# ConvFFN's gate and up projections as two-by-two block products with seven multiplications, in a pass of their own

## The chip, the cores and the metric

One core of one Trainium2 chip runs the kernel. The metric is the time of one execution on the device in microseconds (us); the kernel before took 3261.3 us, the median of 3 runs (3259.72 to 3262.79). Engines are called as in the profile: PE multiplies matrices, PEld loads its weights, DVE, ACT and POOL work on vectors, SP issues DMA transfers.

## The reference

Two layers of a diffusion trunk work on 1024 latent tokens (a 16 x 64 grid) and 128 context tokens with 1024 channels. Layer 0 has a mixer of gated DeltaNet and retention heads, layer 1 a Hyena mixer; each mixer ends in an output projection that is added to the residual x. Behind each stands a ConvFFN with 2816 inner channels, which the change is about:

```python
def conv_ffn(h, w_gate, w_up, w_conv, b_conv, w_down, on_grid):
    gate = h @ w_gate
    up = h @ w_up
    gate = dwconv2d_grid(gate, w_conv) if on_grid else dwconv1d(gate, w_conv[1])
    return (jax.nn.silu(gate + b_conv) * up) @ w_down
...
        hc = modulate(rmsnorm(xc, norm2[l]), mc[3], mc[4])
        hl = modulate(rmsnorm(xl, norm2[l]), ml[3], ml[4])
        xc = xc + mc[5] * conv_ffn(hc, *ffn, on_grid=False)
        xl = xl + ml[5] * conv_ffn(hl, *ffn, on_grid=True)
```

The gate passes a 3x3 depthwise convolution on the grid (three taps on the context). All data is float32.

## The kernel before, in words

Channels lie on the 128 partitions, the 1152 tokens along the free dimension, in NG = 3 groups of G = 384. Every large product is made of three matmuls (`mm3`, lines 134 to 136): each operand is split into a rounded part (hi) and the rest (lo), and hi x hi, hi x lo and lo x hi are summed in PSUM. A weight block is loaded by SP, cast to hi on ACT (line 125) and its lo is a subtraction on DVE (line 126, `wsplit`).

`ffn` (from line 378) goes over 22 blocks of 128 inner channels. `gate(m)` and `up(m)` each run `project`: 3 token groups x 8 blocks of input channels x 3 matmuls of 384 columns. ACT copies the gate out of PSUM (line 384); `conv` does the convolution with 8 instructions of DVE over the grid (line 402) and 2 over the context (line 407), and Silu on ACT. The result of `up` is multiplied in from PSUM on DVE (line 417) and split into hi and lo (lines 418, 419), which stay in SBUF. After each group of blocks (GROUPS, line 37: six groups of up to four) the down projection of that group runs, 8 output blocks x 3 token groups, and `add_x` (line 374) adds each result, scaled, to the residual x in SBUF. The last group goes token group by token group, and the normalisation that follows (`norm_after` or `final`) goes in between.

Ahead of `ffn` stand `out_begin` and `out_end` (lines 802, 849): the mixer's output projection (8 output blocks x 3 token groups x 24 matmuls), `rstd` (line 273; squares on ACT, sums on DVE, a reciprocal root by Newton steps) and `norm_h` (line 305), which writes the normalised, modulated and split operand h. Its scaling on DVE is line 316, splits are lines 321 to 327, some on POOL. The operand of the output projection itself is split at lines 821 and 822. Line 777 is part of the Hyena stage.

`fill` is a list of small pieces of work for the next layer, taken off one at a time by `filler` after each projection and in the down loops: 48 blocks of the modulation (`mod_parts`, line 225; DVE lines 243 and 246) and 8 pieces of the Hyena filter (lines 563 to 569). The order of instructions on each engine is fixed when the kernel is built, from the order in which they are written down and from when their buffers and operands are expected to be ready; buffers come from pools with a fixed number of tiles per tag. All DMA is issued by SP in one order.

## Time and profile before

| | |
|---|---|
| median of 3 runs | 3261.3 us |
| profiled execution, its own time | 3267.89 us |
| its span, first to last instruction | 3266.1 us |
| mean granted TensorE clock | 0.988 of full speed |
| PE, DVE, ACT, POOL busy | 97%, 74%, 32%, 11% |
| first ConvFFN, about | 974 to 1820 us |
| second ConvFFN, about | 2425 to 3252 us |

Times in the trace count from the span's start. A line number is that of the kernel before; where a helper such as `mm3` records every matmul, all stand under its lines, and the names of the tiles (`psg<-hh,wh` is written to PSUM tile `psg` from operand `hh` and weights `wh`) tell them apart. Matmuls overlap in the trace, so the distance between starts is their pace and not the duration of one.

### The profile page before, as it was taken

Reading aid. Unit: us, or ns where it says so; the run is one execution under the profiler, and the core shown is the slowest. Engines: PE = TensorE matmul, PEld = TensorE weight load, DVE = VectorE, ACT = ScalarE, POOL = GpSimd, SP = SyncE. Lnnn points to the kernel's source line nnn. Section 1 sums busy time; section 2 is a strip of 40 time slices with the busy share of each in tenths; the row PEclk is TensorE's granted clock in tenths of the full one; section 3 lists DMA queues with packets and bytes.
Section 4 is the critical chain, followed back from the end, with each engine's and each line's share of the span. In section 5 each row is a group of like instructions: output and inputs, shape, how many; then the busy total and the mean of one; then the engine's idle time right before and its main releaser. Section 6 shows DMA issues by size and latency. Waiting matters only on the chain.

```text
span 3266.1 us, 50005 instructions
## 1 busy us (share of the span) xinstructions
PE 3163.2 (97%) x19856; PEld 3027.5 (93%) x19856; DVE 2406.2 (74%) x5016; ACT 1051.5 (32%) x1889; POOL 369.8 (11%) x406
## 2 busy tenths in 40 slices
...
GB/s 209 69 30 62 62 43 83 39 80 74 131 14 64 90 93 84 78 84 90 79 44 53 179 101 100 109 79 101 154 19 47 39 46 39 46 41 44 45 40 71
DMA packets 84830, 241.38 MB, mean 74 GB/s; under 512 B 10274, under 2 KB 33264, under 8 KB 84596
## 3 DMA queue, kind: packets, MB, share of 16 engines
...
q14 instruction: 78, 0.64, 0.1%
...
## 4 chain that ended last, share of the span: by engine, by line
PE 65%; DVE 7%; issue 1%; DMA 1%; ACT 1%; POOL 0%; DVEq 0%; SPq 0%; ACTq 0%; POOLq 0%
PE psg L134 15%; PE psg L136 15%; PE psg L135 15%; PE psu L134 6%; PE psu L135 6%; PE psu L136 6%; PE psu L656 0%; PE psu L659 0%; PE psu L657 0%; PE psu L658 0%; DVE t L496 0%; PE psu L297 0%; DVE t L497 0%; PE pss L290 0%; DVE x L777 0%
## 5 line engine op out<-in xcount | busy, mean ns | idle before, releaser
L135 PE MATMUL psg<-hl,wh 128*128 128x384 f32 x2400 | 820.0, 342 | 2.7 <-POOL hl L327 2.5
L134 PE MATMUL psg<-hh,wh 128*128 128x384 f32 x2400 | 817.4, 341 | 4.3 <-ACT hh L321 2.6
L136 PE MATMUL psg<-hh,wl 128*128 128x384 f32 x2400 | 818.1, 341 | 0.0
L134 PEld LDWEIGHTS psg<-hh,wh 128*128 128x128 f32 x2400 | 452.7, 189 | 7.3 <-ACT hh L321 3.2
L135 PEld LDWEIGHTS psg<-hl,wh 128*128 128x128 f32 x2400 | 452.9, 189 | 5.6 <-POOL hl L327 5.0
L136 PEld LDWEIGHTS psg<-hh,wl 128*128 128x128 f32 x2400 | 453.1, 189 | 0.0
L402 DVE SCALAR_TENSOR_TENSOR t<-t,vec,t 128x945 f32<-128x945 f32 (+2 forms) x352 | 427.2, 1217 | 23.4 <-ACT t L390 23.4
L125 ACT CAST wh<-wr 128x1024 fp32r<-128x1024 f32 (+1 forms) x192 | 198.6, 1034 | 722.1 <-PE psg L135 627.1
L126 DVE TENSOR_TENSOR wl<-wr,wh 128x1024 fp32r<-128x1024 f32 (+1 forms) x190 | 229.6, 1208 | 255.8 <-ACT wh L125 255.5
L374 DVE SCALAR_TENSOR_TENSOR x<-psg,mod,x 128x384 f32<-128x384 f32 (+2 forms) x444 | 218.0, 513 | 236.4 <-PE psg L136 235.2
L134 PE MATMUL psu<-hh,wh 128*128 128x384 f32 x1056 | 353.0, 334 | 0.0
L136 PE MATMUL psu<-hh,wl 128*128 128x384 f32 x1056 | 353.0, 334 | 0.0
L135 PE MATMUL psu<-hl,wh 128*128 128x384 f32 x1056 | 352.9, 334 | 0.0
L136 PE MATMUL psg<-t,wl 128*128 128x384 f32 x960 | 321.7, 336 | 2.1 <-DVE wl L126 2.1
L134 PE MATMUL psg<-t,wh 128*128 128x384 f32 x960 | 321.7, 335 | 0.0
L135 PE MATMUL psg<-t,wh 128*128 128x384 f32 x960 | 321.4, 335 | 0.0
L134 PEld LDWEIGHTS psu<-hh,wh 128*128 128x128 f32 x1056 | 198.2, 188 | 1.2 <-ACT t L384 0.6
L136 PEld LDWEIGHTS psu<-hh,wl 128*128 128x128 f32 x1056 | 198.2, 188 | 0.8 <-issue 0.6
L135 PEld LDWEIGHTS psu<-hl,wh 128*128 128x128 f32 x1056 | 198.2, 188 | 0.6 <-issue 0.6
L136 PEld LDWEIGHTS psg<-t,wl 128*128 128x128 f32 x960 | 180.9, 188 | 2.5 <-DVE wl L126 2.5
L134 PEld LDWEIGHTS psg<-t,wh 128*128 128x128 f32 x960 | 180.6, 188 | 0.8 <-issue 0.6
L135 PEld LDWEIGHTS psg<-t,wh 128*128 128x128 f32 x960 | 180.6, 188 | 0.0
...
## 6 DMA issues: line engine op xcount, KB each, us to landing
...
```

What stands on the lines that cost most here:

```text
L125: nc.scalar.copy(hi, raw)
L126: (eng or nc.vector).tensor_sub(lo, raw, hi.bitcast(F32))
L134: nc.tensor.matmul(out, lhsT=wh, rhs=xh, start=first and i == 0, stop=False)
L135: nc.tensor.matmul(out, lhsT=wh, rhs=xl, start=False, stop=False)
L136: nc.tensor.matmul(out, lhsT=wl, rhs=xh, start=False, stop=last and i == n - 1)
L374: nc.vector.scalar_tensor_tensor(out=self.x[ob][:, c0:c1], in0=p[:, o], scalar=g, in1=self.x[ob][:, c0:c1], op0=ALU.mult, op1=ALU.add)
L402: nc.vector.scalar_tensor_tensor(out=o, in0=gs[:, r0 + di : r1 + di, c0 + dj : c1 + dj], scalar=w(i, j), in1=o, op0=ALU.mult, op1=ALU.add)
```

## The change

The gate block and the up block of the same 128 inner channels are computed together. The weights are a two-by-two matrix of blocks (rows of the two halves of the input channels; columns gate and up), and h is one too (the two halves of the input channels; even and odd tokens). Instead of the eight products of such a pair, seven are made of sums of blocks (PRODUCTS), and the four results are sums of the seven.

- `out_begin` and `out_end` work on quarters of Q = 288 tokens instead of thirds; weights are loaded and split again for each use. x is kept in halves (`xhalf`) and saved to DRAM (`mid_x`). `norm_ops` takes the place of `norm_h`: it makes B11, B21, B22 and T1 to T4 out of h (four differences per pair of channel blocks, on DVE and POOL) and splits each.
- `pair_weights` loads a gate and an up block and makes S1 to S4 on POOL (three differences and a sum); it splits three tiles of 1024 columns (two on POOL, one on DVE) and one of 512.
- `pair_products` runs the seven products, each over 4 channel blocks x 3 matmuls of 288 columns for one or both halves of the tokens, and sums them: the first is copied out of PSUM on ACT, the others are added from PSUM on DVE, into `y1` (gate) and `y2` (up), every second token.
- `ffn` becomes two passes. The first goes over all 22 blocks (the first two of them in halves), runs `conv`, multiplies by `up` on POOL and stores the product to DRAM (`mid`). The second reads `mid` back, splits it, and runs the down projection in four groups (GROUPS); x is read back too. The fillers are taken three at a time in the down loops of the first three groups, and nowhere else.
- PSUM has 3 + 4 + 1 banks in ConvFFN (3 + 3 + 2 before); weights come from one pool of 9 tiles; `dynamic_dma_scratch_size` goes from 8192 to 1024. `w_down` is laid out in blocks of 128.

```diff
+Q = T // 4
+QP = Q // 2
-NT2 = 7
-NE = 6
+NT2 = 6
+NE = 7
+NW = 9
+NS = 4
-GROUPS = [(0, 2), (2, 6), (6, 10), (10, 14), (14, 18), (18, 22)]
+GROUPS = [(0, 8), (8, 12), (12, 18), (18, 22)]
+
+B11, B21, B22, T1, T2, T3, T4 = range(7)
+PRODUCTS = {1: ("g", "A11", B11), 2: ("u", "A12", B21), 6: ("g", "S2", T2), 3: ("u", "S4", B22),
+            7: ("g", "S3", T3), 4: ("u", "A22", T4), 5: ("u", "S1", T1)}
...
     def open_t2(self, es):
         self.pt2 = es.enter_context(self.tc.tile_pool(name="pt2", bufs=NT2))
+        self.pw = es.enter_context(self.tc.tile_pool(name=self.n("pw"), bufs=NW))
+        self.one = True
+
+    def W(self, shape, dt=F32):
+        return self.pw.tile(list(shape), dt, tag="w", name=self.n("w"))
...
+    def rstd(self, n, order=range(NB), tag="u", pool=(), w=G):
         accs = {}
...
+    def new_ops(self, s):
+
+        def new(t, u):
+            if t == "h":
+                return [self.ph.tile([128, 4, Q], F32R, tag=x, name=self.n("o")) for x in ("hh", "hl")]
+            return [self.pt.tile([128, 4, Q], F32R, tag="t", name=self.n("o")), self.pt2.tile([128, 4, Q], F32R, tag="t2", name=self.n("o"))]
+
+        a = new("h", 0)
+        self.ops[s] = {}
+        for k in range(4):
+            self.ops[s][B11, k] = [t[:, k : k + 1] for t in a]
+        for pair, tags in (((B21, B22), "hh"), ((T1, T3), "ht"), ((T2, T4), "tt")):
+            for h in range(2):
+                t = [x.rearrange("p (k o) c -> p k o c", k=2) for x in new(tags[h], h)]
+                for k in range(2):
+                    self.ops[s][pair, 2 * h + k] = [x[:, k] for x in t]
+                    for o in range(2):
+                        self.ops[s][pair[o], 2 * h + k] = [x[:, k, o : o + 1] for x in t]
+
+    def norm_ops(self, l, which, q, r):
+
+        nc = self.nc
+        s, off = q // 2, QP * (q % 2)
+        if q % 2 == 0:
+            self.new_ops(s)
+        a = self.modA[:, 2 * l + which]
+        sh = self.mod[:, l, 3 * which]
+        v, g = nc.vector, nc.gpsimd
+        for k in range(4):
+            x = []
+            for b in (k, 4 + k):
+                tmp = self.E([128, G])[:, :Q]
+                for c0, c1, st in streams(q * Q, q * Q + Q):
+                    o = slice(c0 - q * Q, c1 - q * Q)
+                    v.scalar_tensor_tensor(out=tmp[:, o], in0=self.xcols(b, c0, c1), scalar=a[:, b, st : st + 1],
+                                           in1=r[:, o], op0=ALU.mult, op1=ALU.mult)
+                    nc.scalar.activation(out=tmp[:, o], in_=tmp[:, o], func=AF.Identity, bias=sh[:, b, st : st + 1])
+                x.append(tmp.rearrange("p (c e) -> p e c", e=2))
+            ta, tb = [self.E([128, G])[:, :Q].rearrange("p (e c) -> p e c", e=2) for _ in range(2)]
+            v.tensor_sub(ta[:, 0], x[0][:, 1], x[0][:, 0])
+            g.tensor_sub(ta[:, 1], x[1][:, 1], x[0][:, 1])
+            v.tensor_sub(tb[:, 0], x[1][:, 1], ta[:, 0])
+            g.tensor_sub(tb[:, 1], x[1][:, 0], tb[:, 0])
+            for key, raw, eng in ((B11, x[0][:, 0:1], v), ((B21, B22), x[1], g), ((T1, T3), ta, v), ((T2, T4), tb, v)):
+                hi, lo = [t[:, :, off : off + QP] for t in self.ops[s][key, k]]
+                self.split(raw, hi, lo, eng)
+
...
+    def pair_weights(self, g_src, u_src):
+
+        nc = self.nc
+        u, g, d = [self.W([128, NB, 128]) for _ in range(3)]
+        nc.sync.dma_start(u, u_src)
+        nc.sync.dma_start(g, g_src)
+        h = [slice(0, 4), slice(4, 8)]
+        sm = lambda dt=F32: self.pw.tile([128, 4, 128], dt, tag="s", bufs=NS, name=self.n("s1"))
+        s1 = sm()
+        e = nc.gpsimd
+        e.tensor_add(s1, u[:, h[0]], u[:, h[1]])
+        e.tensor_sub(d[:, h[0]], s1, g[:, h[0]])
+        e.tensor_sub(d[:, h[1]], g[:, h[1]], d[:, h[0]])
+        e.tensor_sub(u[:, h[0]], g[:, h[0]], u[:, h[0]])
+        s1 = self.split(s1, sm(F32R), sm(F32R), nc.vector)
+        g, d, u = [self.split(t, self.W([128, NB, 128], F32R), self.W([128, NB, 128], F32R), eng)
+                   for t, eng in ((g, e), (d, nc.vector), (u, e))]
+        part = lambda t, i: (t[0][:, h[i]], t[1][:, h[i]])
+        return {"S1": s1, "A11": part(g, 0), "A12": part(g, 1), "S2": part(d, 0), "S4": part(d, 1),
+                "S3": part(u, 0), "A22": part(u, 1)}
+
+    def pair_products(self, w, cols, y1, y2):
+
+        nc = self.nc
+        sums = {s: self.E([128, G])[:, :Q] for s in cols}
+        half = lambda y, s, e: y[:, 2 * Q * s + e : 2 * Q * (s + 1) : 2]
+        add = nc.vector.tensor_add
+        for i, (tag, name, op) in PRODUCTS.items():
+            wh, wl = w[name]
+            for s in cols:
+                p = self.psum(tag, [128, Q])
+                x = self.op(op, s)
+                self.mm3(p, [((wh[:, k], wl[:, k]), x[k]) for k in range(4)])
+                t = sums[s]
+                if i == 1:
+                    nc.scalar.copy(t, p)
+                elif i == 2:
+                    add(half(y1, s, 0), p, t)
+                elif i in (6, 7):
+                    add(t, p, t)
+                elif i == 3:
+                    add(half(y1, s, 1), p, t)
+                elif i == 4:
+                    add(half(y2, s, 0), p, t)
+                else:
+                    add(half(y2, s, 1), p, t)
+                    add(half(y1, s, 1), p, half(y1, s, 1))
...
-        def up(m, acc):
-            hi, lo = self.T(F32R), self.T2(F32R)
-
-            def evac(n, p):
-                c = slice(n * G, n * G + G)
-                nc.vector.tensor_mul(acc[:, c], acc[:, c], p)
-                nc.scalar.copy(hi[:, c], acc[:, c])
-                nc.vector.tensor_sub(lo[:, c], acc[:, c], hi[:, c].bitcast(F32))
-
-            self.project(self.A["w_up"][l, m], "u", evac)
-            return hi, lo
-        gs = [gate(m) for m in range(2)]
-        self.project_first(gs[0][1], gs[1][1])
-        accs = {m: conv(m, gs[m][0]) for m in range(2)}
+
+        mid = self.pd.tile([NFB, 128, T], F32, name=self.n("mid"))
+        plan = [(0, (0,)), (1, (0,)), (0, (1,)), (1, (1,))] + [(m, (0, 1)) for m in range(2, NFB)]
+        blocks, units = {}, []
+
+        def prepare():
+            if len(units) < len(plan):
+                m, cols = plan[len(units)]
+                if m not in blocks:
+                    blocks[m] = (self.X(), self.X())
+                w = self.pair_weights(self.A["w_gate"][l, m], self.A["w_up"][l, m])
+                units.append((w, cols, *blocks[m]))
+
+        prepare()
+        yield
+        for k, (m, cols) in enumerate(plan):
+            prepare()
+            self.pair_products(*units[k])
+            units[k] = None
+            if cols[-1] == 1:
+                g, u = blocks.pop(m)
+                acc = conv(m, g)
+                nc.gpsimd.tensor_mul(acc, acc, u)
+                nc.sync.dma_start(mid[m], acc)
+
+
+        def mids(gi):
+            m0, m1 = GROUPS[gi]
+            out = []
+            for m in range(m0, m1):
+                if gi % 2 == 0:
+                    hi, lo = [self.ph.tile([128, T], F32R, tag=t, name=self.n("mid")) for t in ("hh", "hl")]
+                else:
+                    hi, lo = self.T(F32R), self.T2(F32R)
+                for n in range(NG):
+                    c = slice(n * G, n * G + G)
+                    raw = self.E([128, G])
+                    nc.sync.dma_start(raw, mid[m, :, c])
+                    self.split(raw, hi[:, c], lo[:, c], nc.vector)
+                out.append((hi, lo))
+            return out
+
+        nxt = mids(0)
+        self.x, self.xhalf = [], None
+        for b in range(NB):
+            self.x.append(self.X())
+            nc.sync.dma_start(self.x[b], self.mid_x[b])
         for gi, (m0, m1) in enumerate(GROUPS):
             kb = m1 - m0
-            mids = []
-            for m in range(m0, m1):
-                if m + 1 < NFB and m + 1 not in accs:
-                    g, spec = gate(m + 1)
-                    self.project(*spec)
-                    accs[m + 1] = conv(m + 1, g)
-                mids.append(up(m, accs.pop(m)))
-            last = gi == len(GROUPS) - 1
-
-            def wd(o2, keep=False):
-                src = self.A["w_down"][l, o2, :, 256 * m0 : 256 * m1].rearrange("p (k c) -> p k c", c=256)
-                pool = None
-                if keep:
-                    pool = [new(F32R)[:, : 256 * kb].rearrange("p (k c) -> p k c", c=256) for new in (self.T, self.T2)]
-                return self.wsplit(src, [128, kb, 256], pool)
-
-            def down(w, o2, i, n):
+            cur = nxt
+            if gi + 1 < len(GROUPS):
+                nxt = mids(gi + 1)
+
+            def wd(ob, n):
+                raw = self.W([128, n, kb, 128])
+                for i in range(n):
+                    nc.sync.dma_start(raw[:, i], self.A["w_down"][l, ob + i, :, 128 * m0 : 128 * m1].rearrange("p (k c) -> p k c", c=128))
+                return self.split(raw, self.W([128, n, kb, 128], F32R), self.W([128, n, kb, 128], F32R), nc.vector)
+
+            def down(w, i, ob, n):
                 c = slice(n * G, n * G + G)
-                p = self.psum("g", [128, G])
-                self.mm3(p, [((w[0][:, k, i * 128 : i * 128 + 128], w[1][:, k, i * 128 : i * 128 + 128]),
-                              (mids[k][0][:, c], mids[k][1][:, c])) for k in range(kb)])
-                self.add_x(2 * o2 + i, n, p, l, 5)
-
-            if not last:
-                for o2 in range(4):
-                    w = wd(o2)
-                    if gi:
-                        self.filler()
-                    for i in range(2):
-                        for n in range(NG):
-                            down(w, o2, i, n)
+                p = self.psum("gu"[(ob + n) % 2], [128, G])
+                self.mm3(p, [((w[0][:, i, k], w[1][:, i, k]), (cur[k][0][:, c], cur[k][1][:, c])) for k in range(kb)])
+                self.add_x(ob, n, p, l, 5)
+
+            if gi + 1 < len(GROUPS):
+                for ob in range(NB):
+                    w = wd(ob, 1)
+                    self.filler(3)
+                    for n in range(NG):
+                        down(w, 0, ob, n)
             else:
-                ws = [wd(o2, o2 >= 2) for o2 in range(4)]
+                ws = [wd(ob, 2) for ob in range(0, NB, 2)]
                 for n in range(NG):
-                    for o2 in range(4):
-                        for i in range(2):
-                            down(ws[o2], o2, i, n)
+                    for ob in range(NB):
+                        down(ws[ob // 2], ob % 2, ob, n)
                     after(n)
...
+    def out_end(self, state, l, bcol, close, ffn):
+
+        nc = self.nc
+        fill, weights, block, open_, early = state
+        self.xhalf = [[self.X().rearrange("p (b c) -> p b c", b=2) for _ in range(4)] for _ in range(2)]
...
+        close()
+        self.ops = [None, None]
+        order = [6, 7, 0, 1, 2, 3, 4, 5]
+        self.mid_x = self.pd.tile([NB, 128, T], F32, name=self.n("xmid"))
+
+        def blocks(obs, qs):
+            for ob in obs:
+                w = weights(ob)
+                for q in qs:
+                    block(ob, q, w)
+
+        def save(h):
+            for b in range(NB):
+                nc.sync.dma_start(self.mid_x[b, :, 2 * Q * h : 2 * Q * h + 2 * Q], self.xcols(b, 2 * Q * h, 2 * Q * h + 2 * Q))
+
+        norm = lambda q, r: self.norm_ops(l, 1, q, r)
+        blocks(order[2:], (0, 1))
+        rs = [self.rstd(q, order, w=Q) for q in range(2)]
+        blocks(order[:2], (2,))
+        norm(0, rs[0])
+        blocks(order[2:5], (2,))
+        norm(1, rs[1])
+        save(0)
+        for i in range(NB):
+            fill(i, 3)
+        blocks(order[5:], (2,))
+        r = self.rstd(2, order, w=Q)
+        blocks(order[:2], (3,))
+        norm(2, r)
+        blocks(order[2:5], (3,))
+        next(ffn)
+        blocks(order[5:], (3,))
+        norm(3, self.rstd(3, order, w=Q))
+        save(1)
...
             k.open_ab(e2)
             k.open_psum(e2, g=2, u=3, s=2, x=1)
...
+            ffn = k.ffn(0, k.norm_after(1, 0))

             def close():
                 e2.close()
                 k.open_t2(es)
-                k.open_psum(es, g=3, u=3, s=2)
-
-            k.out_end(out, 0, None, 1, close)
-        k.fill = k.mod_parts(1, range(6), k.T) + k.filter_prepare()
-        k.ffn(0, k.norm_after(1, 0))
-        k.filler(99)
-        k.hyena(1)
-        k.ffn(1, k.final)
+                k.open_psum(e3, g=3, u=4, s=1)
+
+            with ExitStack() as e3:
+                k.out_end(out, 0, None, close, ffn)
+                k.fill = k.mod_parts(1, range(6), k.T) + k.filter_prepare()
+                for _ in ffn:
+                    pass
+                k.filler(99)
+        with ExitStack() as e4:
+            k.open_psum(e4, g=3, u=3, s=2)
+            out = k.hyena(1)
+            ffn = k.ffn(1, k.final)
+
+            def close():
+                e4.close()
+                k.open_psum(es, g=3, u=4, s=1)
+
+            k.out_end(out, 1, V_HBO, close, ffn)
+        for _ in ffn:
+            pass
```

## Rows read from the trace of the kernel before

**Rows 1.** The page, parts 1 and 4: busy time by engine; the chain by engine, line

```profile
PE 3163.2 (97%) x19856; PEld 3027.5 (93%) x19856; DVE 2406.2 (74%) x5016; ACT 1051.5 (32%) x1889; POOL 369.8 (11%) x406
...
PE psg L134 15%; PE psg L136 15%; PE psg L135 15%; PE psu L134 6%; PE psu L135 6%; PE psu L136 6%; PE psu L656 0%; PE psu L659 0%; PE psu L657 0%; PE psu L658 0%; DVE t L496 0%; PE psu L297 0%; DVE t L497 0%; PE pss L290 0%; DVE x L777 0%
```

**Rows 2.** Sums by stretch: PE, PEld, DVE, ACT, POOL busy (instructions), clock, DMA share, GB/s

```profile
860.00:880.00 20.00, 11.72 (x40) 8.86 (x39) 18.06 (x58) 6.87 (x13) 3.06 (x3) 0.64 0.51 174
...
880.00:980.00 100.00, 98.86 (x567) 96.77 (x567) 55.90 (x124) 33.18 (x59) 8.87 (x8) 0.99 0.13 43
1100.00:1600.00 500.00, 500.00 (x2886) 500.00 (x2885) 370.68 (x611) 118.58 (x155) 33.69 (x40) 1.00 0.27 85
2560.00:3160.00 600.00, 600.00 (x3464) 600.00 (x3463) 319.85 (x435) 137.06 (x176) 0.00 (x0) 1.00 0.14 43
```

**Rows 3.** Timeline of PE in the first ConvFFN: start, duration in us, instruction

```profile
1500.16 0.33 PE L134 MATMUL psg<-t,wh 128*128 128x384 f32 x1
...
1505.36 0.33 PE L134 MATMUL psg<-t,wh 128*128 128x384 f32 x1
```

**Rows 4.** Timeline of PE in the Hyena stage, matmuls of 256 columns

```profile
1834.24 0.28 PE L636 MATMUL pss<-e,t 128*128 128x256 f32 x1
...
1834.83 0.28 PE L636 MATMUL pss<-e,t 128*128 128x256 f32 x1
```

**Rows 5.** The page, part 5: groups by line; busy us, mean ns of one, idle before

```profile
L402 DVE SCALAR_TENSOR_TENSOR t<-t,vec,t 128x945 f32<-128x945 f32 (+2 forms) x352 | 427.2, 1217 | 23.4 <-ACT t L390 23.4
...
L374 DVE SCALAR_TENSOR_TENSOR x<-psg,mod,x 128x384 f32<-128x384 f32 (+2 forms) x444 | 218.0, 513 | 236.4 <-PE psg L136 235.2
```

**Rows 6.** Groups of DVE by line and form; busy us, mean ns of one

```profile
L126 DVE TENSOR_TENSOR wl<-wr,wh 128x1024 fp32r<-128x1024 f32 x182 | 224.1, 1231 | 253.2 <-ACT wh L125 252.9
...
L316 DVE SCALAR_TENSOR_TENSOR e<-x,modA,psu 128x384 f32<-128x384 f32 x64 | 37.1, 606 | 3.6 <-PE psu L297 3.5
...
L407 DVE SCALAR_TENSOR_TENSOR t<-t,vec,t 128x127 f32<-128x127 f32 x88 | 30.4, 345 | 0.0
...
L641 DVE TENSOR_TENSOR t<-pss,t 128x512 f32<-128x512 f32 x32 | 21.6, 679 | 1.4 <-PE pss L638 1.4
...
L567 DVE SCALAR_TENSOR_TENSOR e<-e,e 64x384 f32<-64x384 f32 x36 | 19.6, 546 | 0.6
...
L777 DVE TENSOR_TENSOR x<-psu,x 128x512 f32<-128x512 f32 x16 | 18.1, 1136 | 21.3 <-PE psu L771 21.3
...
L126 DVE TENSOR_TENSOR wl<-wr,wh 128x512 fp32r<-128x512 f32 x8 | 5.5, 683 | 2.6 <-ACT wh L125 2.6
...
L644 DVE TENSOR_TENSOR t<-pss,t 128x128 f32<-128x128 f32 x16 | 4.3, 278 | 0.0
```

**Rows 7.** Groups of POOL by line and form

```profile
L327 POOL TENSOR_TENSOR hl<-e,hh 128x384 fp32r<-128x384 f32 x32 | 34.1, 1066 | 394.9 <-ACT hh L326 391.4 <-DMA s<-in_state_delta 2.2 <-issue 1.4
...
L126 POOL TENSOR_TENSOR wl<-wr,wh 128x1024 fp32r<-128x1024 f32 x2 | 4.7, 2344 | 46.1 <-ACT wh L125 46.1
```

**Rows 8.** Timeline of DVE at the end of the Hyena stage

```profile
2297.06 2.02 DVE L693 SCALAR_TENSOR_TENSOR x<-t,vec,x 128x1023 f32<-128x1023 f32 x1
2299.00 2.04 DVE L758 TENSOR_TENSOR t<-t,x 128x1024 f32<-128x1024 f32 x1
2300.96 1.27 DVE L696 SCALAR_TENSOR_TENSOR x<-t,vec,x 128x1023 f32<-128x1023 f32 x1
2302.15 1.51 DVE L759 TENSOR_TENSOR t<-t,t 128x512 f32<-128x512 f32 x1
```

**Rows 9.** Timeline of POOL in the same stretch

```profile
2295.08 4.87 POOL L822 TENSOR_TENSOR y<-e,y 128x384 fp32r<-128x384 f32 x2 [5.46 <-ACT y L821]
2301.00 2.12 POOL L822 TENSOR_TENSOR y<-e,y 128x384 fp32r<-128x384 f32 x1 [1.05 <-ACT y L821]
```

**Rows 10.** Timeline of DVE in one mod block of the first ConvFFN

```profile
1516.96 0.70 DVE L243 SCALAR_TENSOR_TENSOR pss<-wr,t 128x512 f32<-128x512 f32 x1 [3.55 <-DMA wr<-in_mod_w]
...
1519.56 0.08 DVE L246 DVE_READ_ACCUMULATOR wr<-wr,t 128x1 f32 x1
```

186 lines of the change are left out of this document (90 added, 96 removed).

## Prediction

> **What bounds the kernel now.** I read the page first: PE is busy 97% of the span, DVE 74%, ACT 32%, POOL 11%, and the chain that ends last lies first of all in the three matmul lines of `mm3` [rows 1]. A busy PE need not be at its pace, so the sums by stretch come next [rows 2]: 500 us inside the first ConvFFN hold 2886 matmuls and 600 us inside the second 3464, which is 173.2 ns each, with PE busy in every one of them. The timeline says the same: 30 matmuls of 384 columns start within 5.20 us [rows 3]. So ConvFFN lasts as long as its matmuls take to issue, and fewer or narrower ones shorten it as long as nothing else becomes the bound. The same rows show how near the next engine is: DVE is busy 371 of 500 us in the first ConvFFN, which also carries the fillers, and 320 of 600 in the second; POOL does 34 us and nothing. The output projection ahead of ConvFFN (880 to 980) is PE-bound too, 98.9 of 100 us, with DVE at 56.
>
> The sum is made against the profiled execution's own 3267.9 us (span 3266.1), 6.6 above the median of the runs, 3261.3; the difference is then applied to the median.
>
> **Matmuls of the first pass.** A block (128 gate and 128 up channels) had 2 x 3 x 24 = 144 matmuls of 384 columns: 144 x 0.1733 = 24.95 us. After, it has 7 products x 4 k-blocks x 3 terms x 2 token halves = 168 of 288 columns. No row has 288. At 256 columns five starts take 0.59 us, 0.118 each [rows 4]; the line from there to 384 gives 0.1318 (bounds: 0.130, in proportion to columns, and 0.133, all of the overhead kept). 168 x 0.1318 = 22.14 us, 2.81 less, and over 44 blocks **-124 us**, if PE stays the bound. The output projections go from 576 x 0.1733 to 768 x 0.1318, 1.4 us more each: **+3**.
>
> **What DVE and POOL must do in a block.** DVE keeps the 3x3 conv: 8 x 1.217 [rows 5] and 2 x 0.345 [rows 6] = 10.43 us. It splits S1 (512 columns, 0.683) and the S2/S4 tile (1024, 1.231): 1.91. It drains the products: 14 adds of 288 from PSUM. Between 128 columns at 0.278 and 512 at 0.679 [rows 6], 288 cost 0.445 and 384 0.545: 6.23 us for the 14. Ten of the 14 write every second token. The only row with a strided SBUF operand is L777 (every eighth element), 1.136 against 0.679, so the upper bound is 2.7 us more per block; I take the contiguous price, as a step of two is nearer to one than to eight. DVE has 18.6 us of own work in 22.14. ACT stays small: 3.5 casts, two drains and two conv activations. POOL, idle before, gets four sums of 512, two splits of 1024 and the 1152-wide product of conv and up. From 384 at 1.066 to 1024 at 2.344 [rows 7] that is 4 x 1.32 + 2 x 2.34 + 2.60 = 12.57 us.
>
> **Where they meet.** Where both read two SBUF operands, each holds the other up. In the one dense stretch, L693, L758 and L759 took 2.02, 2.04 and 1.51 us on DVE beside 1.27, 1.23 and 0.68 of instructions of that size undisturbed [rows 6, 8]: 2.4 us lost to three POOL instructions [rows 9], 0.8 each, three quarters of the 1.07 such a one takes. So POOL's 12.57 us can cost DVE up to 9.4 a block. Conv and splits are 12.34 of DVE's 18.6 us; the adds have one operand in PSUM, and L316, of that kind, keeps its 0.606 in stages where POOL works [rows 6]. A POOL instruction then meets a sensitive one with a chance between 12.34/24 = 0.51 (DVE partly idle) and 0.66 (never idle): 4.8 to 6.2, DVE at 23.4 to 24.8 us. I take **24.0 us a block**, 0.95 less than before: 44 x 0.95 = **-42 us** in place of -124. The bounds: 22.14 (all of POOL's work falls beside adds and gaps) and 28.0 (all of it delays DVE). Drained late, the products hold seven PSUM banks, about nine tiles of 1.58 us with ACT taking the first two, so conv's burst of 10.4 us alone stops nothing; the sum does.
>
> The Trainium skill (SBUF — State Buffer, "SBUF: two separate sides") states more than these rows: the ports that the two engines share are locked for the whole instruction, and the other one "fully blocks". The rows show three quarters of that, so I price by the rows. By the rule the sum below would be +100 and not +60, which is rival B.
>
> Queues: SP issues 1 MB of weights a block as before, now also behind the store of `mid`, which waits on POOL's product. Behind it stand the weights of the block after next, with half a block of slack by buffer counts, and I cost it at nothing; if that cover is gone, DVE and POOL wait for a load. `mid` and the saved x add about 36 MB in both directions for each layer, under 830 us of which DMA uses 14 to 27% [rows 2]: hidden, except at the seam. The smaller descriptor memory changes no hardware queue that these transfers use: nothing.
>
> **Ahead of the first pass.** DVE's work in one output projection becomes: 24 weight splits (8 before), 29 us; drains, 18; filling the operands, 9; four rstd chains, 22; `norm_ops` 46 (32 scalings, 32 differences of 144, 48 splits at 0.31 to 0.45). That is 125 us, and with the adds and splits of the two half blocks that run meanwhile 135; PE has 101 + 22 = 123. DVE was at 56% there, so the cover is gone: 12 us late, up to 36 where three quarters of POOL's 32 us of differences and splits meet DVE. The first two blocks also run in halves and have their weights prepared twice, 10 us of POOL beside 11 of PE each. I take 15 for each layer, near the lower end because the scalings of `norm_ops` read PSUM, **+30 us** (0 to 80).
>
> **The seam.** Down group 0 needs blocks 0 to 7, read back from DRAM and split. Their buffers still hold the first pass's operands, so some 9 of the 24 splits fit under block 21. After its last matmul DVE owes the conv of block 21 (10.4) and then 15 x 0.545 = 8.2 us of splits: the last operand comes at 19 us, while PE has 72 x 0.1733 = 12.5 us that it can do as they come. So 7 us of stall at least, 19 if in order; **+10 us** in the second layer (5 to 25).
>
> **The first layer's second pass.** The 48 mod blocks and the filter pieces leave the 44 projections and go three at a time into the down loops. A mod block keeps DVE 2.68 us [rows 10]. Down groups 0 and 1 ask of PE 8 x (72 + 36) x 0.1733 = 149.7 us, and of DVE: 47 mod blocks 126, drains 64 x 0.513 = 33, weight splits 15, operand splits 54 x 0.545 = 29, conv of block 21 10: 213, less 5 done early. **+59 us**, seam included (25 to 90). A PE that waits may also be granted less clock: 0.64 with PE busy 11.7 of 20 us [rows 2]. At the lower level group 1's 50 us would be 100, about DVE's 96, so that adds little. Group 2 covers the filter's 30 us or so (36 x 0.546 [rows 6] and as many shorter ones); the last group ends as before. The second layer has no fillers: DVE 130 us under PE's 275.
>
> **Sum:** -42 + 3 + 30 + 10 + 59 = **+60**: 3328 for the profiled execution, 3321 for the median.
>
> **Rivals.** *A, PE stays the bound in the first pass*: POOL's work falls into DVE's gaps. For: after conv DVE waits for PE most of the time, and only 2.6 of 24.9 us need fit. Against: conv follows every block without a gap. Decides where DVE with its waits stays under 22.14 us. -124 + 3 + 59 + 10 and 0 to 30: 3209 to 3239. *B, whole instructions exclude each other*: conv, splits and POOL's work never overlap, 12.34 + 12.57 = 24.9 us a block, no gain in the first pass: -2 + 102 = +100, 3361. The rule named above is this case. For: every delay in that stretch; against: 0.8 of 1.07. *C, all of POOL's price is paid on top of the adds*, since the instruction order was fixed without it: 28.0 us a block, (28.0 - 24.95) x 44 = +134, and +102: 3497. Against: only a dense stretch shows it. *D, the fillers go where DVE is free*, and the 59 becomes nothing: 3262, no change. Against: the two row tiles that they hold throughout are among the six that the operands occupy in the first pass. That the products are not saved is excluded: the loops issue 168 x 288 columns in place of 144 x 384.
>
> **Chances.** Forecast 0.38 (own range 3275 to 3385), A 0.31, B 0.15, C 0.08, D 0.08, half of it "same", half faster. A measurement of this kernel can tell about 0.2%, 6.5 us. Faster 0.35 (A and half of D), same 0.06 (the other half and the forecast's edge), slower 0.59. The range 3205 to 3415 takes in the forecast, A, B and D and leaves out C and the far ends.
>
> **What would show it.** Right: a block of the first pass takes 24 us with PE gaps behind DVE's adds; conv instructions grow from 1.22 us where POOL works; in the first layer's groups 0 and 1 DVE is near 100% and PE at 70%; a stall of 10 us at the seam. Wrong: 12 matmuls per 1.58 us throughout the first pass (A), conv instructions and POOL's that never overlap (B), a block over 26 us (C), PE full under the fillers (D), or a DVE that waits for loads at the seam.

## The result, and the profile after

The changed kernel takes 3633.4 us (median of 4 runs, 3631.7 to 3637.6) beside 3262.0 for the kernel before in the same session: ratio 1.114, 95% interval 1.112 to 1.116. It is slower, as forecast, but by 371 us and not by 60, far outside the range. Its page, parts 1 and 4, against [rows 1]:

```profile
PE 3176.6 (88%) x21320; PEld 3014.5 (83%) x21320; DVE 2853.7 (79%) x5628; ACT 1169.3 (32%) x2141; POOL 1104.5 (30%) x808
...
DVE 9%; PE 9%; POOL 3%; issue 3%; DMA 2%; ACT 2%; POOLq 0%; SPq 0%; DVEq 0%; ACTq 0%
```

PE no longer makes up the chain almost alone: the chain is followed back only over the last 28% of the span here, and in it PE and DVE have 9% each. Sums by stage say where the time came from. First comes the kernel before, with the stretches from the first output projection's full pace to ConvFFN, ConvFFN, Hyena, second projection, second ConvFFN (columns as in [rows 2]); then the same stretches of the kernel after.

```profile
874.00:974.00 100.00, 99.01 (x553) 96.73 (x552) 56.47 (x118) 31.57 (x55) 7.27 (x7) 0.96 0.16 52
974.00:1816.00 842.00, 837.95 (x4790) 827.70 (x4789) 630.72 (x1080) 235.01 (x346) 54.85 (x66) 1.00 0.25 79
1816.00:2335.00 519.00, 494.61 (x3277) 483.05 (x3276) 460.73 (x765) 185.38 (x310) 55.48 (x49) 0.99 0.33 114
2335.00:2436.00 101.00, 99.72 (x575) 97.65 (x574) 57.69 (x131) 37.02 (x71) 10.19 (x10) 0.99 0.12 41
2436.00:3266.00 830.00, 818.07 (x4719) 815.90 (x4717) 476.81 (x704) 202.18 (x279) 3.81 (x6) 0.99 0.14 46
```

```profile
874.00:1057.00 183.00, 121.41 (x798) 117.17 (x799) 124.09 (x259) 81.83 (x171) 59.89 (x62) 0.82 0.34 113
1057.00:2012.00 955.00, 828.43 (x5252) 802.47 (x5251) 784.19 (x1235) 243.17 (x348) 364.22 (x212) 0.93 0.31 103
2012.00:2558.00 546.00, 494.91 (x3276) 483.58 (x3276) 459.83 (x768) 186.90 (x318) 64.00 (x49) 0.96 0.31 106
2558.00:2740.00 182.00, 123.42 (x843) 119.53 (x844) 130.04 (x272) 86.26 (x184) 65.92 (x68) 0.84 0.34 112
2740.00:3630.00 890.00, 793.32 (x5195) 781.87 (x5193) 630.62 (x867) 212.00 (x290) 316.64 (x150) 0.95 0.24 78
```

The projections grew by 83 and 81 us, ConvFFN by 113 and 60, Hyena by 27: 364 us, the difference of the spans. In ConvFFN the last product of the first pass starts at 1637.7 and 3315.5 us. Taking 22 blocks at the old pace (549 us by [rows 2]) as what each first pass replaces, the first passes cost 31 and 26 more, the second passes 82 and 34. (78 and 123 of a pass's 3696 products, 10 and 16 us, already run inside the projections' stretches, so that as much of the first row below belongs to the second.)

| term | forecast | measured |
|---|---|---|
| output projections and norm | +33 | +164 |
| first passes | -42 | +57 |
| first layer's second pass, seam included | +59 | +82 |
| second layer's seam | +10 | +34 |
| Hyena | 0 | +27 |

**One block of the first pass.** DVE, then POOL, in the kernel after, over the head of one conv:

```profile
1299.34 1.20 DVE L532 SCALAR_TENSOR_TENSOR x<-x,vec,x 128x945 f32<-128x945 f32 x1 [2.70 <-ACT x L520]
1300.46 1.38 DVE L537 SCALAR_TENSOR_TENSOR x<-x,vec,x 128x127 f32<-128x127 f32 x1
1301.76 2.25 DVE L532 SCALAR_TENSOR_TENSOR x<-x,vec,x 128x960 f32<-128x960 f32 x1
1303.93 1.38 DVE L537 SCALAR_TENSOR_TENSOR x<-x,vec,x 128x127 f32<-128x127 f32 x1
1305.23 3.33 DVE L532 SCALAR_TENSOR_TENSOR x<-x,vec,x 128x945 f32<-128x945 f32 x1
1308.48 0.45 DVE L500 TENSOR_TENSOR x<-psu,e 128x288 f32<-128x288 f32 x1
...
1335.08 0.45 DVE L500 TENSOR_TENSOR x<-psu,e 128x288 f32<-128x288 f32 x1
```

```profile
1300.35 1.34 POOL L474 TENSOR_TENSOR w<-s,w 128x512 f32<-128x512 f32 x1 [2.95 <-DMA w<-in_w_gate]
1301.65 1.34 POOL L476 TENSOR_TENSOR w<-w,w 128x512 f32<-128x512 f32 x1
1302.95 2.21 POOL L475 TENSOR_TENSOR w<-w,w 128x512 f32<-128x512 f32 x1
1305.12 2.43 POOL L153 TENSOR_TENSOR w<-w,w 128x1024 fp32r<-128x1024 f32 x1
```

The two take turns, whole instruction by whole instruction. A tap of 127 elements (0.345 in [rows 6]) takes 1.38 us because it waits for POOL's L474; L475 takes 2.21 because it waits for a tap; the last tap waits out the split that began at 1305.12 and runs only then. Five taps sum to 9.54 us in place of 4.3. POOL begins these sums as `in_w_gate` lands, and SP's rows show why that falls on the head of the conv:

```profile
1295.38 0.33 SPq L565 DMA_DIRECT2D mid<-x  x1
1295.76 1.18 SPq L468 DMA_DIRECT2D w<-in_w_gate  x1
```

The load is issued right behind the store of `mid`, and that store goes out as POOL's product of the conv before it ends (1295.36). So the end of one conv sets when the next unit's sums start. Over both layers, in 31 of the 40 blocks in which they run the five taps sum to 9.5 to 9.6 us. Where the sums begin 2.5 us behind the head of the conv (the block at 1194 us) the five taps take 5.3 us; later taps are held up instead, and PE waits 0.5 us at the place read next, and 1.9 us further on.

Behind the taps stand the adds (L500, L502) that free PSUM. So PE runs out of banks; its row, and the sums by 2 us around it:

```profile
1312.06 0.40 PE L161 MATMUL psg<-o,w 128*128 128x288 f32 x1 [2.63 <-DVE e L502]
1312.30 0.39 PE L162 MATMUL psg<-o,w 128*128 128x288 f32 x1
```

```profile
1312.00:1314.00 2.00, 1.94 (x9) 1.94 (x10) 2.00 (x4) 0.00 (x0) 0.00 (x0) 0.59 0.00 0
1314.00:1316.00 2.00, 2.00 (x11) 2.00 (x11) 2.00 (x3) 0.00 (x0) 0.11 (x1) 0.56 0.04 8
1316.00:1318.00 2.00, 2.00 (x17) 2.00 (x17) 2.00 (x5) 1.10 (x1) 2.00 (x1) 1.00 0.00 0
```

After the wait PE is granted about the lower level, 1.2 GHz, and its starts lie 0.24 us apart and not 0.13, for 16 matmuls: 1.7 us more. 22.14 as priced, 2.63 of waiting and 1.7 of slow clock make 26.5; the rows of L500 say 26.60. Over 500 us of the first pass the granted clock is 0.94, where [rows 2] has 1.00:

```profile
1100.00:1600.00 500.00, 439.29 (x3111) 432.86 (x3112) 424.94 (x490) 127.72 (x153) 282.10 (x133) 0.94 0.19 63
```

The Trainium skill (SBUF — State Buffer, "SBUF: two separate sides") states this exclusion for a VectorE instruction with two SBUF inputs beside a GpSimd one that reads SBUF, or for one in a two-port mode, and for no other. The trace agrees for both kinds: the taps above wait, and the adds, with one operand in PSUM, take 0.46 us at most where POOL works beside them.

### The profile page after: what moved, and what is told of

Read it like the earlier page. It is cut to its first block, busy times and chain, and to the rows that moved or that the text cites. A ratio compares the mean times of both kernels' runs of the same rounds, so it can differ in the third digit from the quotient of the medians.

```text
span 3629.9 us, 55385 instructions
## 1 busy us (share of the span) xinstructions
PE 3176.6 (88%) x21320; PEld 3014.5 (83%) x21320; DVE 2853.7 (79%) x5628; ACT 1169.3 (32%) x2141; POOL 1104.5 (30%) x808
## 5 line engine op out<-in xcount | busy, mean ns | idle before, releaser
L532 DVE SCALAR_TENSOR_TENSOR x<-x,vec,x 128x945 f32<-128x945 f32 (+2 forms) x352 | 557.5, 1584 | 115.7 <-ACT x L520 115.7
L152 ACT CAST w<-w 128x1024 fp32r<-128x1024 f32 (+2 forms) x270 | 268.4, 1010 | 740.6 <-POOL w L153 232.2
L161 PE MATMUL psg<-o,w 128*128 128x288 f32 x1056 | 329.9, 312 | 119.0 <-DVE e L502 115.3
L153 POOL TENSOR_TENSOR w<-w,w 128x1024 fp32r<-128x1024 f32 x96 | 270.4, 2817 | 326.5 <-DVE w L153 320.9
L163 PE MATMUL psg<-o,w 128*128 128x288 f32 x1056 | 325.9, 309 | 8.7 <-POOL w L153 8.7
L162 PE MATMUL psg<-o,w 128*128 128x288 f32 x1056 | 325.3, 308 | 0.0
L161 PE MATMUL psu<-o,w 128*128 128x288 f32 x1056 | 321.1, 304 | 0.0
L162 PE MATMUL psu<-o,w 128*128 128x288 f32 x1056 | 319.1, 302 | 0.0
L163 PE MATMUL psu<-o,w 128*128 128x288 f32 x1056 | 318.2, 301 | 0.0
L161 PEld LDWEIGHTS psg<-o,w 128*128 128x128 f32 x1056 | 210.1, 199 | 128.8 <-DVE e L502 124.6
L161 PE MATMUL psg<-hh,wh 128*128 128x384 f32 x768 | 272.5, 356 | 2.8 <-ACT hh L356 2.2
L162 PE MATMUL psg<-hl,wh 128*128 128x384 f32 x768 | 272.2, 355 | 2.6 <-POOL hl L362 2.6
L163 PE MATMUL psg<-hh,wl 128*128 128x384 f32 x768 | 272.8, 356 | 0.0
L163 PEld LDWEIGHTS psg<-o,w 128*128 128x128 f32 x1056 | 212.0, 201 | 9.7 <-POOL w L153 9.7
L162 PEld LDWEIGHTS psg<-o,w 128*128 128x128 f32 x1056 | 211.6, 200 | 0.0
L161 PEld LDWEIGHTS psu<-o,w 128*128 128x128 f32 x1056 | 208.2, 197 | 0.0
L162 PEld LDWEIGHTS psu<-o,w 128*128 128x128 f32 x1056 | 207.4, 196 | 0.0
L163 PEld LDWEIGHTS psu<-o,w 128*128 128x128 f32 x1056 | 206.0, 195 | 0.0
```

The source lines that it names most:

```text
L152: self.nc.scalar.copy(hi, raw)
L153: eng.tensor_sub(lo, raw, hi.bitcast(F32))
L161: nc.tensor.matmul(out, lhsT=wh, rhs=xh, start=first and i == 0, stop=False)
L162: nc.tensor.matmul(out, lhsT=wh, rhs=xl, start=False, stop=False)
L163: nc.tensor.matmul(out, lhsT=wl, rhs=xh, start=False, stop=last and i == n - 1)
L532: nc.vector.scalar_tensor_tensor(out=o, in0=gs[:, r0 + di : r1 + di, c0 + dj : c1 + dj], scalar=w(i, j), in1=o, op0=ALU.mult, op1=ALU.add)
```

## Experiments

Single runs, but for e12 and e17 (medians of 4); the kernel before took 3262 to 3267 beside them. "Projection" runs from its first matmul to the first product, "second pass" from the last product to the last store of x (first layer) or to the end.

| kernel | program | projection | first pass | second pass |
|---|---|---|---|---|
| after | 3633 | 209, 183 | 613, 615 | 375, 314 |
| e1_pool_free | 3387 | 199, 180 | 509, 509 | 369, 299 |
| e2_sums_dve | 3588 | 210, 183 | 593, 592 | 374, 314 |
| e3_chopped | 3681 | 208, 186 | 635, 632 | 380, 318 |
| e4_norm_plain | 3613 | 201, 179 | 611, 608 | 374, 318 |
| e5_w_ahead | 3630 | 207, 187 | 612, 609 | 376, 316 |
| e6_fill_even | 3638 | 207, 183 | 610, 610 | 390, 315 |
| e7_seam | 3600 | 208, 184 | 608, 611 | 363, 304 |
| e8_last2 | 3665 | 207, 190 | 609, 613 | 393, 330 |
| e9_ffn_late | 3597 | 195, 171 | 610, 614 | 373, 314 |
| e10_one_weight | 3572 | 185, 161 | 609, 607 | 373, 314 |
| e11_sums_after | 3587 | 209, 183 | 595, 591 | 373, 315 |
| e12_combined | 3532 | 194, 172 | 589, 583 | 369, 301 |
| e13_free_combined | 3355 | 195, 171 | 505, 504 | 359, 298 |
| e14_half_fill | 3588 | 209, 184 | 613, 609 | 336, 314 |
| e15_last_one | 3626 | 210, 184 | 609, 614 | 371, 315 |
| e16_all_dve | 3534 | 205, 183 | 574, 571 | 370, 311 |
| e17_combined_all | 3492 | 196, 171 | 570, 572 | 364, 300 |

### The first pass: GpSimd beside VectorE

**e1**, in `pair_weights`:

```diff
-        e.tensor_add(s1, u[:, h[0]], u[:, h[1]])
...
-        g, d, u = [self.split(t, self.W([128, NB, 128], F32R), self.W([128, NB, 128], F32R), eng)
-                   for t, eng in ((g, e), (d, nc.vector), (u, e))]
+        s1 = self.split(u[:, h[1]], sm(F32R), sm(F32R), nc.vector)
+        d = self.split(u, self.W([128, NB, 128], F32R), self.W([128, NB, 128], F32R), nc.vector)
+        g, u = [(hi, hi) for hi in (self.W([128, NB, 128], F32R), self.W([128, NB, 128], F32R)) for _ in (nc.scalar.copy(hi, g),)]
```

> Leaves out the four weight sums and the two low-half splits that GpSimd makes for each block of the first pass (the products read plain and rounded weights instead); matmuls, adds, conv taps and ScalarE casts stay; the final product of gate and up stays on GpSimd. Theory A (a VectorE and a GpSimd instruction exclude each other as wholes; the sums fall on the conv's first taps, the product adds behind the taps come late, TensorE stalls some 2.8 us and restarts at the lower clock): the taps fall back to about 1.2 and 0.3 us, the stall goes, a block takes 22 us instead of 26.6, the program about 3633 - 44 x 4.5 = 3435 us. Theory B (the cause is the order of VectorE's queue: products of 288 columns leave TensorE only some 10 us of lead over a conv of 10 us, whatever GpSimd does): the stall stays, a block takes at least 25.5 us, the program is at or above 3590 us.

3387 us, 246 less. DVE's timeline of one block, for the same taps (L526 and L531 here):

```profile
1302.34 1.20 DVE L526 SCALAR_TENSOR_TENSOR x<-x,vec,x 128x945 f32<-128x945 f32 x1 [0.88 <-ACT x L514]
1303.46 0.34 DVE L531 SCALAR_TENSOR_TENSOR x<-x,vec,x 128x127 f32<-128x127 f32 x1
1303.72 1.21 DVE L526 SCALAR_TENSOR_TENSOR x<-x,vec,x 128x960 f32<-128x960 f32 x1
...
1324.61 1.20 DVE L526 SCALAR_TENSOR_TENSOR x<-x,vec,x 128x945 f32<-128x945 f32 x1 [0.88 <-ACT x L514]
```

A block takes 22.27 us, PE is busy without a break, and theory B falls: 7 banks are lead enough for a conv of 10 us. 22.27 is also the priced 22.14, so the pitch of 288 columns was right. This run takes six tiles of the weight pool for a unit in place of nine, so it does not separate GpSimd's work from the pool by itself; e16 below keeps all nine.

**e2** moves the four sums and leaves the splits of g and u on GpSimd, **e11** asks for the next unit behind the conv as well, **e16** moves the splits too:

```diff
-        e = nc.gpsimd
+        e = nc.vector
...
-                   for t, eng in ((g, e), (d, nc.vector), (u, e))]
+                   for t, eng in ((g, nc.gpsimd), (d, nc.vector), (u, nc.gpsimd))]
```

The second change is e2's and e11's alone. e11 also:

```diff
-            prepare()
             self.pair_products(*units[k])
...
                 nc.sync.dma_start(mid[m], acc)
+            prepare()
```

> The four weight sums of a block move from GpSimd to VectorE; GpSimd keeps two splits and the final product; all work is done. Theory A (exclusion at the conv's first taps): VectorE gets 4 x 0.69 = 2.8 us more of its own and loses some 5 us of waiting for GpSimd, a block takes about 24 us, the program about 3633 - 44 x 2.4 = 3530 us. Theory B (VectorE's own load and order set the pace): a block takes 26.6 us or up to 2.8 more, the program 3633 to 3750 us.

> As the run with the weight sums on VectorE (3587 us), and the next unit's weights are asked for behind the conv, not ahead of the products, so that the sums stand behind the conv's taps on VectorE. Theory A (in that run VectorE stood 3.2 us per block at a sum that waited for its weight's transfer, with the taps behind it): that idle time goes, a block takes about 23.5 us instead of 25.6, the program about 3500 us. Rival (the buffers let the weights in no sooner, and the splits then come late for TensorE): a block takes 25.6 us or more, the program 3587 us or above.

> All of the weight work of the first pass on VectorE, the four sums and all splits; GpSimd keeps the product of conv and up; nothing is left out. VectorE's own work in a block grows from 18.6 to 18.6 + 4 x 0.69 + 2 x 1.22 = 23.8 us, the most of all versions. Theory A (a VectorE instruction of two SBUF operands waits for a whole GpSimd one): the taps and splits fall back to 1.2 us but for two or so beside the product, a block takes 24 to 25 us instead of 26.6 (25.6 with the sums alone moved), the program 3510 to 3570 us. Rival (VectorE's own load is the bound, and each addition to it costs): a block takes more than 26.6 us, the program above 3633 us.

e2 gave 46 us, less than half of what its theory A expected. e11 gave the same 46, so its theory A fell: moving the sums in the queue took most of VectorE's wait away (3.2 us in the block read in e2, 1.0 in e11), but a tap then ran 3.36 us and a split 2.62 beside the two splits left on POOL. e16, which gives DVE the most to do, is the fastest of the three: 3534 us, 99 less. Its taps, with POOL doing only the product:

```profile
1301.45 1.20 DVE L532 SCALAR_TENSOR_TENSOR x<-x,vec,x 128x945 f32<-128x945 f32 x1
1302.56 0.35 DVE L537 SCALAR_TENSOR_TENSOR x<-x,vec,x 128x127 f32<-128x127 f32 x1
...
1325.79 1.20 DVE L532 SCALAR_TENSOR_TENSOR x<-x,vec,x 128x945 f32<-128x945 f32 x1
```

24.3 us for this block, 24.9 on average. So collisions, not VectorE's load, held the pace of the kernel after. In e16 VectorE's longer queue does count: PE waits 81 us in the two first passes for the first add (L500), and a block is still 2.6 us behind e1.

**e3**, the same work in pieces (the other sums, the two splits and the product likewise):

```diff
+CH = 2
...
-        e.tensor_add(s1, u[:, h[0]], u[:, h[1]])
...
+        for i in range(0, 4, CH):
+            a, b = slice(i, i + CH), slice(4 + i, 4 + i + CH)
+            e.tensor_add(s1[:, a], u[:, a], u[:, b])
...
```

> The same work on the same engines, but each GpSimd instruction of the first pass is cut into pieces of 256 elements per partition (sums of 512 into two, splits of 1024 into four, the product of 1152 into five). Theory A (whole instructions take turns): a tap waits for one piece of about 0.65 us instead of 1.3 to 2.4 us, the five first taps end some 3 us sooner, the stall shrinks, a block takes about 24.3 us, the program about 3633 - 44 x 2.2 = 3535 us, and GpSimd's work takes longer. Rival (the two engines share the port at reduced rates): the taps stay as long, a block takes 26.6 us or more, the program 3633 us or above.

A miss: 3681 us, 47 more. Yet the taps did shrink, as whole turns demand and shared rates don't. POOL, then DVE (L544 and L549 are the taps here):

```profile
1313.94 0.79 POOL L478 TENSOR_TENSOR w<-w,w 128x256 f32<-128x256 f32 x1
1314.69 1.65 POOL L477 TENSOR_TENSOR w<-s,w 128x256 f32<-128x256 f32 x1
```

```profile
1314.05 1.70 DVE L544 SCALAR_TENSOR_TENSOR x<-x,vec,x 128x960 f32<-128x960 f32 x1
1315.67 0.82 DVE L549 SCALAR_TENSOR_TENSOR x<-x,vec,x 128x127 f32<-128x127 f32 x1
```

A tap waits for one piece (1.70 and not 2.25 or 3.33), but a piece waits for a tap each time, and POOL's weight work ended later. DVE then stood 1.7 us at the split of d, waiting for ACT's cast, with the product adds behind it, and PE 2.19 us behind those. The loss changed its place.

### The output projections

**e4** leaves out the four differences of `norm_ops`, **e5** loads the next weights ahead of the norm:

```diff
-            v.tensor_sub(ta[:, 0], x[0][:, 1], x[0][:, 0])
...
+            ta, tb = x
```

```diff
...
+        a = ahead(order[2:5])
         norm(0, rs[0])
-        blocks(order[2:5], (2,))
+        run(a, 2)
...
```

> Leaves out the four differences of norm_ops (two on VectorE, two on GpSimd, for each of 4 pairs of channel blocks and 4 token quarters); the splits read the normed tiles directly, so all splits, casts and matmuls stay. Theory A (the weights' casts stand on ScalarE behind the operands' casts, which wait for GpSimd's and VectorE's differences, and TensorE waits for the weights): the output projections shrink from 183 and 178 us to 130 to 145 each, the program to about 3550 us. Theory B (the reload of the weights, 24 loads, casts and subtractions in place of 8, sets the pace through its buffers): each projection stays above 165 us, the program above 3605 us.

> In out_end the weights of the next three output blocks are loaded and split ahead of norm_ops of the first, second and third token quarter, not behind it; all else stays. Theory A (the weights' casts stand behind the norm's casts on ScalarE, and these wait for VectorE and GpSimd): the 19.5 us gap of TensorE at 988 us and its like in the other layer go to under 5 us, each output projection gets 15 to 25 us shorter, the program about 3590 us. Theory B (buffers decide: three sets of weights in the pool, and the last quarter's operands, which can only be loaded once the first half's residual has been normed and saved): the gaps move and stay, the program within 10 us of 3633.

Both theories A fell: 12 us of both projections together in e4, nothing in e5. What PE waits for in the kernel after stands in its three longest gaps, and SP's issues show what lay between the first two:

```profile
967.07 1.09 PE L161 MATMUL psg<-y,w 128*128 128x288 f32 x3 [12.72 <-ACT y L977]
...
1007.92 0.61 PE L161 MATMUL psg<-y,w 128*128 128x288 f32 x1 [19.20 <-ACT w L152]
...
1055.58 0.58 PE L161 MATMUL psu<-o,s 128*128 128x288 f32 x1 [10.56 <-DVE e L447]
```

```profile
976.75 0.38 SPq L137 DMA_DIRECT2D w<-in_ab_wo  x1
979.09 4.41 SPq L1039 DMA_DIRECT2D xmid<-x  x2
983.60 0.38 SPq L467 DMA_DIRECT2D w<-in_w_up  x1
984.08 0.39 SPq L468 DMA_DIRECT2D w<-in_w_gate  x1
991.82 6.36 SPq L1039 DMA_DIRECT2D xmid<-x  x2
1000.60 0.33 SPq L137 DMA_DIRECT2D w<-in_ab_wo  x1
```

Between two output weights the first unit's gate and up weights are loaded; with their splits they need nine tiles of a pool of nine. The next output weight comes 24 us later. **e9** moves that unit:

```diff
-        next(ffn)
         blocks(order[5:], (3,))
         norm(3, self.rstd(3, order, w=Q))
+        next(ffn)
```

> The first unit's pair_weights is asked for behind the last output blocks and the last quarter's norm, not between the output blocks of the last quarter. Theory A (the nine buffers of the shared weight pool: the unit takes all nine, so that the output weights behind it wait until GpSimd has split the unit's): TensorE's gap of 19.5 us in the last quarter goes to under 5 us, the weights of the first unit come up to 10 us later, the output projections get some 10 us shorter each, the program about 3613 us. Rival (the gap is the norm's, whatever is loaded): the program at or above 3633 us.

37 us less, 26 of them in the projections; the gap of 19.2 fell to 1.8 and 6.1. The gap of 12.7 stayed (14.3): the last quarter's operands need the tiles of the first half's residual, which are free when `norm(1)` and `save(0)` are done, and are loaded by way of tiles that `norm(1)` uses too (SP waits 13.5 us for its casts and differences between 930 and 970 us). The third gap is the norm of the last quarter, on VectorE: PE has run out of products of the first half. It is 10.6 and 12.1 us in the two layers and stays in e9 (10.4) and e10 (10.0). In e4, whose norm is shorter, both these gaps are gone in both layers, but waits for weights (7.6 and 10.1 to 10.3 us) stand in place of most of the gain. So the norm holds PE, and with less norm the weights do.

**e10**, in `out_end`:

```diff
-                w = weights(ob)
+                w = weights(ob) if 0 in qs else fixed
...
+        fixed = weights(order[0])
```

> Leaves out the reload of the output weights for the third and fourth token quarters: all 16 of their blocks multiply by one weight that is loaded once; matmuls, additions and norm_ops stay. Theory A (the reloads: 16 loads, casts and subtractions per layer in queues and buffers that the norm uses as well): both large gaps of TensorE (13 and 19.5 us) mostly go, each output projection gets 35 us or more shorter, the program about 3560 us. Theory B (norm_ops sets the pace: VectorE is busy 18 of 20 us while it works, and the last quarter's operands wait for the first half's norm): the 13 us gap stays, each projection gets 10 to 20 us shorter, the program about 3605 us.

24 and 22 us less per projection, between the theories; the gap at the last quarter's operands stays (11 us). So reloads, the unit in the shared pool, the tiles of the last quarter and its norm all hold PE. What the first two are worth together was not tried.

### The second pass and Hyena's start

**e7** loads two weights early and asks for the second group's products later:

```diff
+        early = [wd(0, ob, 1) for ob in range(2)]
         nxt = mids(0)
...
-                    w = wd(ob, 1)
+                    w = early.pop(0) if early else wd(gi, ob, 1)
+                    if ob == 2:
+                        nxt = mids(gi + 1)
```

> In the second pass the first two weights are loaded ahead of the products' reload, and the second group's products are asked for behind the second block of outputs, not at the start; all bytes are still moved. Theory A (SyncE's queue: the weight of the second output block is asked for behind the reload of the residual and of two groups of products): TensorE's gap of 18.8 us in the first layer and of 10 us in the second go to under 4 us, the program about 3603 us. Theory B (bandwidth: 4.7 MB of products and 4.7 MB of residual have to land at some 300 GB/s before the first additions): TensorE waits as long for something else, the program within 10 us of 3633.

33 us less, 12 and 10 of them in the second passes by the table. In the kernel after, the second weight is issued behind the reloads, and PE waits for its cast:

```profile
1678.84 0.59 SPq L598 DMA_DIRECT2D w<-in_w_down  x1
```

```profile
1689.29 0.69 PE L161 MATMUL psg<-mid,w 128*128 128x384 f32 x1 [18.48 <-ACT w L152]
```

In e7 that wait is 11.8 us; in the second layer it was 11.5 us and is gone. So the order of issues is shown as a part of it. That the rest in the first layer is transfers is not shown, but fits: DMA's share between 1640 and 1700 is 0.89, at 308 GB/s, in the kernel after, and as high in e7 (0.88 from 1630 to 1690).

**e6**, and **e14** in `mod_parts`:

```diff
-                    self.filler(3)
+                    self.filler((3, 1 + ob % 2, 3)[gi])
```

```diff
-            for i in range(2):
...
-            nc.gpsimd.tensor_add(self.mod[:, l, j, b, 0:1], half[:, 0, 0:1], half[:, 1, 0:1])
...
+            nc.gpsimd.tensor_copy(self.mod[:, l, j, b, 0:1], self.mod[:, l, j, b, 1:2])
```

> Fillers of the first layer's second pass: 3 per block of outputs in the first group as before, 1 or 2 in turn in the second (its products take TensorE half as long), 3 in the third. Theory A (in the second group VectorE's share of fillers is more than TensorE's work there, so that the split weights come late; the third group has room): the gaps of 2.6 to 5.6 us at each output block from 1783 to 1860 us go, with the slower clock behind them, the stage from the last product of the first pass to Hyena goes from 375 to about 350 us, the program to about 3608 us. Rival (the same work is late in the third group): 370 to 378 us, the program 3628 us or more.

> Leaves out the fillers' products for the first stream (two of 0.69 us and their reads of 0.14 us for each of 48 rows, 80 us of VectorE); GpSimd copies the second stream's sum in their place. Theory A (in the first layer's second pass VectorE with the fillers is the bound of the second group and of the seam before it): the stage from the last product of the first pass to Hyena goes from 375 to 330 us or less (the second layer's, without fillers, takes 314 with the final norm), the program about 3588 us. Rival (transfers and weights set the pace there): 365 us or more, the program above 3620 us.

e6 missed: the stage grew by 15 us. Yet the second group took 65 us and not 86, as its theory A wanted, the third 108 and not 99. What undid it is the last group, 80 us and not 54: there PE waits 5.9, 5.7 and 7.0 us for the norm's sums behind each token group, where the kernel after has one such wait, at the end. Why that changed stays open. e14 is 39 us shorter in this stage (45 in all), and the 39 lie in the first three groups, 33 of them in the second. So VectorE's filler work is what PE waits for there. The sums by stretch of the kernel after show the place. The first stretch lies in the first group; the second holds most of the second group (1769 to 1855 us) and the head of the third; the last holds the rest of the third and of the last group:

```profile
1700.00:1780.00 80.00, 80.00 (x464) 80.00 (x462) 78.45 (x179) 13.93 (x24) 15.75 (x21) 1.00 0.61 197
1780.00:1880.00 100.00, 68.64 (x285) 63.88 (x285) 84.46 (x199) 12.51 (x23) 11.02 (x22) 0.76 0.44 153
1880.00:1995.00 115.00, 114.97 (x624) 104.97 (x623) 78.80 (x163) 36.29 (x63) 4.11 (x4) 1.00 0.17 50
```

In the first stretch DVE is full and PE just fed; in the second PE does 285 matmuls in 100 us (577 at the old pace), a share of them at the lower clock.

**e8** and **e15**:

```diff
-GROUPS = [(0, 8), (8, 12), (12, 18), (18, 22)]
+GROUPS = [(0, 8), (8, 12), (12, 20), (20, 22)]
...
-                ws = [wd(ob, 2) for ob in range(0, NB, 2)]
+                ws = [wd(ob, 4) for ob in range(0, NB, 4)]
...
```

```diff
-                ws = [wd(ob, 2) for ob in range(0, NB, 2)]
+                ws = [wd(0, 2)] * (NB // 2)
```

> Groups of the second pass of 8, 4, 8 and 2 rows in place of 8, 4, 6 and 4: the last group's weights then fill 4 buffers of the shared weight pool and not 8. Theory A (Hyena's first weights can't be loaded before the last group's products end, because these weights hold 8 of the 9 buffers): TensorE's idle time at Hyena's start (27 of 40 us from 2000 us on) mostly goes, Hyena's weights land before the last group ends, the program about 3613 us. Rival (TensorE waits there for the norm of the last token group, whatever the weights do): within 8 us of 3633.

> In the last group of the second pass one weight of two output blocks serves all eight (three loads, casts and subtractions left out per layer), which frees six of the nine buffers of the weight pool earlier. Theory A (Hyena's first weights wait for these buffers, and with them TensorE at Hyena's start): its first weight is asked for before 1970 us instead of 2003, TensorE's idle 27 us there shrink to under 12, the program about 3613 us. Rival (TensorE waits for the last token group's norm): the idle time stays, the program within 8 us of 3633.

e8 missed, 31 us slower: a last group of two rows gives PE too little under each token group's norm (it waits 9.2 and 10.6 us for the norm's sums). In e15 Hyena's first weight was asked for at 1932 us (2003 before), and PE's idle time there stayed. The kernel after:

```profile
2016.73 1.44 PE L317 MATMUL pss<-ones,e 128*128 128x2 f32 x6 [6.14 <-DVE e L310]
2020.68 1.62 PE L324 MATMUL psu<-ident,rs 128*128 128x128 f32 x6 [2.51 <-DVE rs L298]
2032.86 0.55 PE L788 MATMUL pss<-e,t 128*128 128x256 f32 x1 [10.55 <-DVE e L351]
```

In e15 these waits are 5.4, 2.5 and 8.9 us. The pool is not the cause. In the kernel before, PE ran Hyena's input products (`psg<-hh`) from 1813 us, around the last norm; after, the filter's spectrum (L788) stands first in its queue. That this order is the cause is read from the traces and was not tested, and why the built order differs stays open.

### Together

**e12** is e2, e7 and e9 in one; **e13** is e1, e7 and e9; **e17** is e16, e7 and e9.

> All three mends that helped by themselves, with all work done: the weight sums on VectorE (by itself 3587 us), the first weights of the second pass and the second group's products in another order (3600 us), and the first unit asked for behind the output blocks (3597 us). If the three are independent, 3633 - 46 - 33 - 37 = 3517 us. If they mend the same loss, it stays above 3560 us. In either case slower than the kernel before the change by 7% or more.

> The run without GpSimd's weight work (3387 us, the sums and two splits left out) with the two other mends. If what is left of the loss lies in the output projections, the seams and the fillers, 3387 - 33 - 37 = 3317 us; that would still be above the kernel before at 3262 us, so that even without the exclusion the change would not pay. If the mends overlap with the weight work left out, 3350 us or more.

> The last run's kernel with the two other mends (first weights of the second pass early, first unit behind the output blocks), all work done. Against 3532 us with the two splits left on GpSimd: if a block takes 24.5 us, 3532 - 44 x 1 = 3490 us; if VectorE's load is the bound, at or above 3532 us.

e12: 3532 us (4 runs; ratio to before 1.083, 1.081 to 1.085). e17: 3492 us (4 runs; 1.070, 1.068 to 1.072), all work done: 142 us of the 371 come back, and the change still loses. 3490 was expected for a block of 24.5 us; its blocks take 24.9. e13: 3355 us and not 3317, so the mends are worth less together; even with GpSimd's weight work gone that is 92 us more than before. No version beats the kernel before.

## Why the prediction was right and wrong

**Right**: the bound and its pace; 288 columns at 0.1318 (22.27 against 22.14 us a block); strided adds at the contiguous price (0.445 forecast and measured); POOL's sums and splits (1.34 and 2.43 against 1.32 and 2.34); "conv's burst of 10.4 us alone stops nothing" (e1); and VectorE as the bound under the fillers (e14). The sign of the whole came out too, partly by luck: the first passes were to gain 42 us and lost 57, and the terms that were to lose were all too small.

**"Where they meet"** failed first. The step priced a meeting at three quarters of POOL's instruction and let it happen by chance, for 24.0 us a block. The block takes 26.4 on average (448.6 us for the last 17 of the first layer, from S1 product to S1 product): turns are whole, the sign that the prediction had set down for rival B, and they do not fall by chance. [rows 9] already showed the other half of each turn: POOL's three instructions took 4.87 us for two and 2.12, twice the 1.07 that the prediction gives such a one, so they had waited too; it read only DVE's loss. The transfer that releases POOL's sums lands within 1.1 us behind the head of the conv in most blocks, where the lost 5 us delay the adds that PE needs. Rival B had the mechanism but its price, 24.9, was a sum of busy times; the wait of PE and the slow clock after it were in neither. Without GpSimd's weight work (e1) the first passes are 210 us shorter. "A PE that waits may also be granted less clock ... so that adds little" was argued for one stage only; here it is 1.7 us of the block read, and 240 and 263 of the 3696 products of the first passes start 0.2 to 0.3 us behind the one before.

**"Ahead of the first pass"** failed most: +33 for both layers became +164. It added up the work of DVE (135 us) and PE (123) as if either could run on, and took the 12 us between them. PE's work fits; what it misses are buffers. The first unit takes all nine tiles of the shared pool (e9), 16 weights more are loaded and split in the same pool (e10), and the last quarter's operands wait for tiles that the first half's norm must free. DVE, busy 124 of 183 us, was not the bound of the stage; only at its end does PE wait for DVE, 10.6 and 12.1 us for the last quarter's norm, near the 12 of the sum, which stood for something else.

**"The first layer's second pass"** had the right mechanism (e14) and too small a size: 82 for 59, since the seam cost more and PE, waiting in the second group, ran part of it at the lower clock.

**"The seam"** counted DVE's splits and left out SP's order: the weight of the second output block is issued behind two sets of reloads (e7). 34 us in the second layer for 10; 11.5 of them are the wait for that weight, and e7 gives 10 back. What else is in the 34 no run separates. **"Queues"**, costed at nothing with half a block of slack, is this same miss, and it reaches into the first pass: there the load of `in_w_gate` behind the store of `mid` keeps POOL waiting 48 of 500 us.

**Hyena** was given nothing. Its 27 us are idle time of PE (busy 494.9 of 546 us, 494.6 of 519 before), 18 of them in the three waits at its start; the cause is open.
